# A hybrid encoder trunk on one core: first head by token halves, moved gate products, and factor rows by identity products

## The chip, the cores and the metric

The kernel runs on one core of one Trainium2 chip. Times are device microseconds (us) of one execution of the whole program; of several executions the median is given. A profile is one such execution, taken with the hardware profiler; its span runs from the first to the last instruction of the core.

## The reference, cut to what matters

x is 1024 tokens of 1024 features in float32. Two layers follow each other, each with a mixer and a SwiGLU feed-forward part (width 2816), each part behind an RMS norm and added to x; a last RMS norm ends it.

```python
hn = rmsnorm(x, norm_mix_w[i])                  # x * rsqrt(mean(x*x) + eps) * w
x = x + mlstm_mixer(hn, ...)                    # layer 0;  layer 1: window_attn_mixer
x = x + swiglu(rmsnorm(x, norm_ffn_w[i]), ...)
```

The mLSTM mixer has 4 heads. One product of hn gives for each head q and k (128 features each), v (256), an output gate (256, through a sigmoid), and 16 gate rows for all heads. Each head runs over 8 chunks of 128 tokens, forward and backward, with a state that is carried from chunk to chunk:

```python
s = einsum(q, k) * exp(D - m_t)                 # within the chunk, masked
num = einsum(s, v) + inter * einsum(q, C_prev)  # C_prev: state of the chunks before
h = num / max(|den|, exp(-m_t))
hs = h_fwd + h_bwd
hs = hs * rsqrt(mean(hs*hs) + eps) * norm_w
return (hs * o_gate) @ w_out
```

The attention mixer has 16 heads with windows of 128 tokens, rotary positions and one learned sink value for each head, which enters the maximum and the denominator of the softmax.

## The kernel before, in words

All activations are kept transposed: a tile of x holds 128 features on the partitions and 1024 tokens along the row, so that 8 tiles (`self.x`) hold x. Products go over two halves of 512 tokens. Every float32 operand of a large product is split into a rounded high part and a rest (`split`, `split_scaled`: the high part on ACT, the rest on DVE), and three products (high·high, high·rest, rest·high) make one exact one (`three`). A product of 1024 features into 128 for one half is 24 matmul instructions (`product`). Weights are cut the same way (`cut`: `wh` on ACT at line 187, `wl` on POOL at line 188), and their loads (`feed`, `raw`) run two tiles ahead on the SP queue, in the order that `sources` lists. Most of SBUF is one pool of 46 buffers of 128x1032 words (`unit`); a tile waits for a buffer until an older one is released. x, the normalised tiles (16 buffers, `hnh` and `hnl`), the weights and the per-head data all live there.

The code is written as lists of small steps, which `weave` lays into each other: main steps with filler products between them. The order of the instructions of each engine is fixed when the program is built, by a list scheduler that starts from the order in the code and moves an instruction up where its inputs and buffers are there by estimated times. At run time each engine works its list in order. So code of a later phase can stand early in an engine's list if nothing holds it back: `attn_setup` belongs to the first feed-forward phase (`run`), but its masks and the line-1353 negation of the sinks have tiles of their own in the constant pool, so they need no buffer of the phase before.

Norms: `norm_begin` takes rows R (128 x 1024, the factor of each token on every partition) and `rcol` (the factor of each token down the partitions). `norm_split` (lines 204, 205) makes `hnh` and `hnl` without the factor; products are multiplied by R when they leave PSUM. The sums of squares are summed over partitions by a product with ones (`norm_sums`, line 364), `rsqrt` takes the power -0.5 on POOL (line 353) and two Newton steps on DVE, `spread` (lines 370 to 384) makes R from `rcol`: eight small DVE instructions for 512 tokens build diag(rcol) as a high part and a rest (lines 376, 377), and two products with ones (lines 381, 382) spread it, then ACT copies it into R (line 383). `last_out` uses `spread` for the final norm, in parts of 512, 256 and 256 tokens.

The mLSTM phase (`mlstm`, line 1058): x is loaded (line 240), ACT's list is held to the order of the code while the two halves are split; `norm_direct` makes the sums of squares: the squares of half 0 and two of half 1 on POOL (line 305), six of half 1 on ACT (line 303), the adds on DVE and POOL (lines 306 to 310). The gate rows are 48 products with only 16 output rows (tile `pn`, line 228). Then head 0's features: q, k, and the two gate blocks, each for half 0 then half 1 (`m_in`, 8 products of 24 matmuls), with `norm_sums` and `norm_rows` called between their parts and the gates' long chain (`gates`) advanced at given places (`marks`). From then on the loop over heads weaves the 34 steps of head hh (`m_mix`: `state`, `step`, `prep`) with the 64 feature parts of head hh+1. The last head has no next head: there, with `a, b = 4, 6`, its steps run alone for six steps, while the finished heads 0 and 1 are loaded back (`take_back`, line 711, and their splits at lines 200 and 201), x is loaded again, and the output product (`out_pair`) of heads 0 and 1 fills the rest.

The attention phase (`attn`) weaves 32 units of softmax work with the rotary products of the later query groups (`qs`) by the table `plan`, and with the output products from unit 21 on.

Of the kernel before, what the change touches and what calls it, by code (L numbers as in the profile page):

```python
# [11 lines left out]
F32 = mybir.dt.float32  # L12
# [69 lines left out]
class Trunk:  # L82
# [58 lines left out]
    def sources(self):  # L141
        h = self.h
        cols = lambda src: [src[:, o:o + D] for o in range(0, src.shape[-1], D)]
        out = [h["m_gate"]]
        for u in range(3 * NH):
            out += cols(h["m_in"][u])
        for u in range(4):
            out += cols(h["m_out"][u])
        ffn = [[], []]
        for i in range(2):  # L150
            for f in range(NF):
                ffn[i] += cols(h["ffn_in"][i, f])
            for f0, f1 in FF_CHUNKS:
                ffn[i] += [h["ffn_out"][i, d, :, f0 * P:f1 * P] for d in range(KT)]
        att = []
        for u in range(6):
            att += cols(h["a_in"][u])
        for u in range(4):
            att += cols(h["a_out"][u])
        return out + ffn[0] + att + ffn[1]  # L160
# [134 lines left out]
    def norm_direct(self, half):  # L295
        nc = self.nc
        V, G = nc.vector, nc.gpsimd
        a, b = (self.slab() for _ in range(2))
        for d in range(KT):
            x = self.xv(d, half)  # L300
            sq = (b if d % 2 else a)[:, d // 2 * HALF:(d // 2 + 1) * HALF]
            if half and d < 6:
                nc.scalar.activation(sq, x, AF.Square)
            else:
                G.tensor_tensor(sq, x, x, op=ALU.mult)
        V.tensor_tensor(a[:, :S], a[:, :S], b[:, :S], op=ALU.add)
        G.tensor_tensor(a[:, S:], a[:, S:], b[:, S:], op=ALU.add)
        yield
        V.tensor_tensor(a[:, :S], a[:, :S], a[:, S:], op=ALU.add)
        V.tensor_tensor(self.Rv(half), a[:, :HALF], a[:, HALF:S], op=ALU.add)  # L310
        yield
# [36 lines left out]
    def rsqrt(self, out, ss, n, tag, w):  # L348
        nc = self.nc
        v = self.t([P, w], F32, tag + "v", 2)  # L350
        g = self.t([P, w], F32, tag + "g", 2)
# [18 lines left out]
    def spread(self, t, n):  # L370
        nc = self.nc
        hi, lo = (self.t2(F32R)[:, :n] for _ in range(2))
        for j in range(n // P):
            o = slice(j * P, (j + 1) * P)
            r = self.rcol[:, t // P + j:t // P + j + 1]
            nc.vector.tensor_scalar(hi[:, o], self.ident, r, None, op0=ALU.mult)
            nc.vector.scalar_tensor_tensor(
                lo[:, o], self.ident, r, hi[:, o].bitcast(F32), op0=ALU.mult, op1=ALU.subtract
            )
        rb = self.bank("mx")[:, :n]  # L380
        nc.tensor.matmul(rb, lhsT=self.ones_r, rhs=hi, start=True, stop=False)
        nc.tensor.matmul(rb, lhsT=self.ones_r, rhs=lo, start=False, stop=True)
        nc.scalar.activation(self.R[:, t:t + n], rb, AF.Copy)
        return rb
# [51 lines left out]
    def norm_end(self):  # L436
        sums = lambda: [self.norm_sums(half) for half in range(2)]
        rows = lambda: [self.norm_rows(half) for half in range(2)]
        self.pending = [sums, rows]
# [411 lines left out]
    def m_in(self, hh, t):  # L851
# [4 lines left out]
        def feature(unit, w, half):  # L856
            dst = lambda: t["qk" if unit == 0 else "so"][:, w * S + half * HALF:w * S + (half + 1) * HALF]

            def pairs():
                if w == 0 and half == 0:  # L860
                    t["qk" if unit == 0 else "so"] = self.slab()
                if half == 0:
                    st["w"] = self.w()
                else:
                    self.ahead()
                return self.dense_pairs(st["w"], half)
# [25 lines left out]
        fs = sum((feature(u, w, half) for u in range(2) for w in range(2) for half in range(2)), [])  # L892
        return fs, self.v_parts(value)
# [164 lines left out]
    def mlstm(self):  # L1058
        nc, h = self.nc, self.h
        with ExitStack() as es:  # L1060
# [6 lines left out]
            with self.tc.manual_schedule(engines={mybir.EngineType.Activation}):  # L1067
                sums = [self.norm_direct(half) for half in range(2)]
                for half in range(2):
                    for d in range(KT):  # L1070
                        self.norm_split(d, half)
                        if half and d == 4:
                            next(sums[0])
                    next(gates)
                    next(sums[half])
                next(sums[1])
# [3 lines left out]
            marks = (11, 16, 28, 36, 44)  # L1080
            norms = [lambda: self.norm_sums(0), lambda: self.norm_rows(0), lambda: self.norm_sums(1), lambda: self.norm_rows(1)]
            for i, f in enumerate(ins[0][0]):
                if i in (1, 3, 4, 7):
                    norms.pop(0)()
# [3 lines left out]
            weave(mix[0][0], ins[0][1])  # L1088
            y01, y2 = [[], []], []
            for hh in range(NH):  # L1090
                early, steps, late, y = mix[hh]
                if hh + 1 < NH:
                    weave(steps, ins[hh + 1][0])
                    nxt = mix[hh + 1][0]
                    both = [late[0], nxt[0], late[1], late[2], nxt[1], late[3], late[4], nxt[2], nxt[3]]
                    weave(both, ins[hh + 1][1])
                else:
                    backs = [self.take_back(self.ykeep[j], y01[j]) for j in range(2)]
                    self.load_x(h["x"])
                    back = lambda: self.take_back(self.ykeep[2], y2)()  # L1100
                    idle = [lambda: None]
                    a, b = 4, 6
                    weave(steps[:a] + backs + steps[a:b])
# [233 lines left out]
    def attn_setup(self):  # L1337
# [12 lines left out]
        self.sink = self.const.tile([P, 16], F32, name="sink")  # L1350
        nc.sync.dma_start(self.sink, self.h["sink"])
        self.nsink = self.const.tile([P, 16], F32, name="nsink")
        V.tensor_scalar(self.nsink, self.sink, -1.0, None, op0=ALU.mult)

    def attn(self):
# [8 lines left out]
        with self.phase("a", 6, dict(mm=3, sc=2, tp=2, mx=1)):  # L1364
# [17 lines left out]
            plan = ((0, nq), (4, len(qs) // 3), (11, 2 * len(qs) // 3), (19, len(qs)), (n + 3, len(qs)))  # L1382
# [126 lines left out]
```

## Time and profile before

| | us |
|---|---|
| median of 3 runs | 2332.02 |
| lowest and highest | 2330.37, 2334.89 |
| the profiled execution | 2334.53 |
| its span | 2332.8 |

The mean granted TensorE clock is 0.982 of full speed. PE is busy for 2228.1 us of the span, PE's weight loads for 1826.9, DVE for 1421.6, ACT for 832.8, POOL for 608.7. In the rows further down a time in front is the start from the beginning of the span and the next number the duration, "x8" a count of instructions, and the bracket how long the engine had been idle before and which engine, tile and line released it. A matmul's recorded duration includes the modelled drain, so the spacing of matmuls is read from a run of them: (duration of the run minus one drain) over the count.

### The profile page before, as it was taken

What the parts mean: (1) busy time and instruction counts of PE and PEld (TensorE: products, weight loads), DVE (VectorE), ACT (ScalarE), POOL (GpSimd) and SP (SyncE); (2) the same over time, 40 slices, a digit from 0 to 9 for tenths busy, and PEclk for the clock granted to TensorE, in tenths of its full rate; (3) what the DMA queues carried; (4) which work ended last, traced back from release to release, by engine and by line L of the source; (5) the groups of instructions that cost most, each with busy time, mean ns of one, the idle gap of its engine ahead of it and who ended that gap; (6) DMA issues with size and microseconds to landing.
All of it is one profiled execution on the core that took longest, in us unless ns stands there. A gap on an engine that the chain in (4) does not pass through costs nothing.

```text
span 2332.8 us, 28234 instructions
## 1 busy us (share of the span) xinstructions
PE 2228.1 (96%) x10655; PEld 1826.9 (78%) x10655; DVE 1421.6 (61%) x2603; ACT 832.8 (36%) x1533; POOL 608.7 (26%) x410
## 2 busy tenths in 40 slices
PE   6999998989999999999999998898999999999998
PEld 3889888867888888778878776786788888878887
DVE  5456656678766666592224689878766666653113
ACT  3334445344222222222222577764322222232021
POOL 4312213221111111231343455550111111133043
PEclk9999999998999999999999999999999999999999
DMA  3211114122222222622222444603222222263112
GB/s 114 58 37 46 52 49 145 55 99 82 82 82 82 82 81 77 229 97 86 92 89 85 130 132 135 206 10 116 74 82 81 82 82 82 74 240 119 46 55 73
DMA packets 75961, 216.77 MB, mean 93 GB/s; under 512 B 8320, under 2 KB 14976, under 8 KB 75824
## 3 DMA queue, kind: packets, MB, share of 16 engines
q1 hardware_dynamic: 64216, 177.07, 23.3%
q10 hardware_dynamic: 11608, 37.89, 4.1%
q8 instruction: 84, 1.38, 0.2%
q14 instruction: 53, 0.43, 0.1%
HBM read 159.15 MB, written 55.77 MB: 92 GB/s over the span
## 4 chain that ended last, share of the span: by engine, by line
PE 77%; DVE 8%; issue 5%; DMA 4%; POOL 2%; ACT 2%; SPq 1%; POOLq 0%; ACTq 0%; DVEq 0%
PE mm L532 37%; PE mm L628 18%; PE mm L228 12%; PE mm L476 4%; PE pn L212 2%; DMA raw<-in_a_in_dram 1%; PE sc L1271 1%; POOL wl L188 1%; DVE smd L1286 1%; PE pk L212 1%; DMA slab<-bounce 1%; PE tp L1300 1%; PE mx L1315 1%; ACT e L1280 1%; DVE e L1276 1%
## 5 line engine op out<-in xcount | busy, mean ns | idle before, releaser
L188 POOL TENSOR_TENSOR wl<-raw,wh 128x1024 fp32r<-128x1024 f32 (+2 forms) x96 | 233.7, 2439 | 594.0 <-ACT wh L187 391.2
L628 PE MATMUL mm<-hh,wl 128*128 128x512 f32 (+1 forms) x768 | 289.9, 378 | 4.6 <-POOL wl L188 4.6
L628 PE MATMUL mm<-hh,wh 128*128 128x512 f32 (+1 forms) x768 | 289.0, 379 | 4.3 <-ACT hh L200 3.2
L628 PE MATMUL mm<-hl,wh 128*128 128x512 f32 (+1 forms) x768 | 289.9, 377 | 1.1 <-DVE hl L201 1.1
L579 POOL TENSOR_TENSOR t<-t,R 128x512 f32<-128x512 f32 x44 | 57.4, 1305 | 613.6 <-ACT t L578 613.6
L628 PEld LDWEIGHTS mm<-hh,wh 128*128 128x128 f32 x768 | 145.4, 189 | 34.4 <-ACT hh L200 4.0
L628 PEld LDWEIGHTS mm<-hh,wl 128*128 128x128 f32 x768 | 145.3, 189 | 34.4 <-POOL wl L188 5.9
L628 PEld LDWEIGHTS mm<-hl,wh 128*128 128x128 f32 x768 | 145.5, 189 | 30.3 <-DVE hl L201 1.9
L655 DVE TENSOR_TENSOR x<-x,mm 128x512 f32<-128x512 f32 x80 | 54.6, 685 | 178.2 <-PE mm L628 178.0
L228 PE MATMUL mm<-slab,wh 128*128 128x512 f32 x512 | 152.8, 407 | 6.1 <-ACT wh L187 3.1
L578 ACT ACTIVATE t<-t 128x512 f32<-128x512 f32 x44 | 27.8, 632 | 330.9 <-DVE t L577 330.9
L532 PE MATMUL mm<-f12h,wbh 128*128 128x512 f32 x352 | 138.9, 395 | 0.0
L532 PE MATMUL mm<-f12l,wbh 128*128 128x512 f32 x352 | 138.7, 394 | 0.0
L532 PE MATMUL mm<-f12h,wbl 128*128 128x512 f32 x352 | 138.7, 394 | 0.0
L570 DVE TENSOR_TENSOR t<-mm,t 128x512 f32<-128x512 f32 x44 | 30.4, 691 | 159.9 <-PE mm L532 159.9
L187 ACT ACTIVATE wh<-raw 128x1024 fp32r<-128x1024 f32 (+3 forms) x106 | 102.1, 969 | 71.9 <-DVE hl L201 56.1
L228 PE MATMUL mm<-hnh,wh 128*128 128x512 f32 x416 | 124.6, 399 | 0.9 <-DVE x L655 0.9
L228 PE MATMUL mm<-hnl,wh 128*128 128x512 f32 x416 | 124.5, 401 | 0.0
L228 PE MATMUL mm<-hnh,wl 128*128 128x512 f32 x416 | 124.1, 398 | 0.0
L532 PE MATMUL mm<-f,wah 128*128 128x512 f32 x352 | 113.0, 403 | 10.8 <-DVE x L692 10.8
L532 PE MATMUL mm<-f34h,wd 128*128 128x512 f32 x352 | 117.6, 394 | 0.0
L228 PEld LDWEIGHTS mm<-slab,wh 128*128 128x128 f32 x512 | 95.9, 193 | 26.8 <-ACT wh L187 4.1
(296 smaller groups left out, 5318.7 us busy)
## 6 DMA issues: line engine op xcount, KB each, us to landing
raw<-in_ffn_in_dram SPq DMA_DIRECT2D x88, 512.0 KB
hkeep<-hs ACTq DMA_DIRECT2D x44, 512.0 KB
hraw<-hkeep SPq DMA_DIRECT2D x44, 512.0 KB
raw<-in_ffn_out_dram SPq DMA_DIRECT2D x32, 512.0 KB
raw<-in_m_in_dram SPq DMA_DIRECT2D x24, 512.0 KB
xkeep<-x ACTq DMA_DIRECT2D x24, 512.0 KB
x<-xkeep SPq DMA_DIRECT2D x48, 256.0 KB
bounce<-slab SPq DMA_DIRECT2D x40, 256.0 KB
```

The lines of the kernel that those rows point to most:

```text
L187: nc.scalar.activation(hi[:, c], r[:, c], AF.Copy)
L188: (nc.vector if fast else nc.gpsimd).tensor_tensor(lo[:, c], r[:, c], hi[:, c].bitcast(F32), op=ALU.subtract)
L212: self.nc.tensor.matmul(out, lhsT=l, rhs=r, start=start and i == 0, stop=stop and i == len(jobs) - 1,)
L228: self.nc.tensor.matmul(st["ps"], lhsT=l, rhs=r, start=j == 0, stop=j == len(jobs) - 1)
L476: self.nc.tensor.matmul(st[c], lhsT=l, rhs=r, start=j == 0 and a == 0, stop=j == 1 and a == len(jobs) - 1)
L532: self.nc.tensor.matmul(ps, lhsT=l, rhs=r, start=start and j == 0, stop=stop and j == len(jobs) - 1, skip_group_check=True,)
L570: V.tensor_tensor(u2, pb, p1, op=ALU.add)
L578: A.activation(g0, g0, AF.Silu)
L579: G.tensor_tensor(g0, g0, R0, op=ALU.mult)
L628: nc.tensor.matmul(po, lhsT=l, rhs=r, start=j == 0, stop=j == len(jobs) - 1)
L655: V.tensor_tensor(x, x, po, op=ALU.add)
L1271: T.matmul(ps[:, :n], lhsT=lq, rhs=kk[:, j * S + k0 * P:j * S + (k0 + nk) * P], start=j == 0, stop=j == 1,)
```

## The change

Six edits. (1) The sinks are loaded into a tile of the feed-forward phase's own pool and copied from there. (2) `norm_direct` goes; `norm_half` splits one half and then squares it, all eight squares on ACT, with the adds on DVE. (3) Head 0's first four products run q half 0, k half 0, q half 1, k half 1; the marks are moved to suit. (4) The last head's gate products (`ins[hh][1]`, 32 parts, 96 matmuls) leave the steps of head 2 and stand in the last head's steps 0 to 7; the reload of heads 0 and 1 is issued after the first 16 parts, their splits and the reload of x come after all 32. (5) `spread` multiplies each column of `rcol`, broadcast, with the identity, in plain float32: four products for 512 tokens, no DVE work; `rsqrt`'s scratch tiles have one buffer each. (6) In `attn` the rotary filler that ended at unit 19 ends at unit 21.

```diff
-        for u in range(3 * NH):
+        for u in list(range(3 * NH - 2)) + [3 * NH - 1, 3 * NH - 2]:
             out += cols(h["m_in"][u])
...
+    def norm_half(self, half):
+        V = self.nc.vector
         for d in range(KT):
+            self.norm_split(d, half)
+        q = [self.unit(name="sq") for _ in range(4)]
+        for d in range(KT):
+            o = d % 2 * HALF
+            self.nc.scalar.activation(q[d // 2][:, o:o + HALF], self.xv(d, half), AF.Square)
+        for i, j in ((0, 1), (2, 3), (0, 2)):
+            V.tensor_tensor(q[i], q[i], q[j], op=ALU.add)
+        V.tensor_tensor(self.Rv(half), q[0][:, :HALF], q[0][:, HALF:], op=ALU.add)
...
-        v = self.t([P, w], F32, tag + "v", 2)
-        g = self.t([P, w], F32, tag + "g", 2)
+        v, g = (self.t([P, NC], F32, tag + x, 1)[:, :w] for x in "vg")
...
     def spread(self, t, n):
         nc = self.nc
-        hi, lo = (self.t2(F32R)[:, :n] for _ in range(2))
+        rb = self.bank("mx")[:, :n]
         for j in range(n // P):
-            o = slice(j * P, (j + 1) * P)
-            r = self.rcol[:, t // P + j:t // P + j + 1]
-            nc.vector.tensor_scalar(hi[:, o], self.ident, r, None, op0=ALU.mult)
-            nc.vector.scalar_tensor_tensor(
-                lo[:, o], self.ident, r, hi[:, o].bitcast(F32), op0=ALU.mult, op1=ALU.subtract
+            c = t // P + j
+            nc.tensor.matmul(
+                rb[:, j * P:(j + 1) * P], lhsT=self.rcol[:, c:c + 1].broadcast_to([P, P]), rhs=self.ident,
+                start=True, stop=True,
             )
-        rb = self.bank("mx")[:, :n]
-        nc.tensor.matmul(rb, lhsT=self.ones_r, rhs=hi, start=True, stop=False)
-        nc.tensor.matmul(rb, lhsT=self.ones_r, rhs=lo, start=False, stop=True)
         nc.scalar.activation(self.R[:, t:t + n], rb, AF.Copy)
...
-        fs = sum((feature(u, w, half) for u in range(2) for w in range(2) for half in range(2)), [])
-        return fs, self.v_parts(value)
+        order = [(u, w, half) for u in range(2) for w in range(2) for half in range(2)]
+        if hh == 0:
+            order[1], order[2] = order[2], order[1]
+        fs = [feature(*o) for o in order]
+        return sum(fs[:4], []), sum(fs[4:], []), self.v_parts(value)
...
-                sums = [self.norm_direct(half) for half in range(2)]
                 for half in range(2):
-                    for d in range(KT):
-                        self.norm_split(d, half)
-                        if half and d == 4:
-                            next(sums[0])
+                    self.norm_half(half)
                     next(gates)
-                    next(sums[half])
-                next(sums[1])
...
-            marks = (11, 16, 28, 36, 44)
+            marks = (13, 20, 36, 42, 47)
...
-                if i in (1, 3, 4, 7):
+                if i in (1, 5, 9, 13):
                     norms.pop(0)()
...
-                    weave(steps, ins[hh + 1][0])
+                    weave(steps, ins[hh + 1][0] + (ins[hh + 1][1] if hh + 2 < NH else []))
...
-                    backs = [self.take_back(self.ykeep[j], y01[j]) for j in range(2)]
-                    self.load_x(h["x"])
...
-                    a, b = 4, 6
-                    weave(steps[:a] + backs + steps[a:b])
+                    a, b, o = 4, 8, ins[hh][1]
+                    weave(steps[:a], o[:16])
+                    backs = [self.take_back(self.ykeep[j], y01[j]) for j in range(2)]
+                    weave(steps[a:b], o[16:])
+                    for f in backs:
+                        f()
+                    self.load_x(h["x"])
...
-        self.sink = self.const.tile([P, 16], F32, name="sink")
-        nc.sync.dma_start(self.sink, self.h["sink"])
-        self.nsink = self.const.tile([P, 16], F32, name="nsink")
-        V.tensor_scalar(self.nsink, self.sink, -1.0, None, op0=ALU.mult)
+        raw = self.t([P, 16], F32, "sink", 1)
+        nc.sync.dma_start(raw, self.h["sink"])
+        self.sink, self.nsink = (self.const.tile([P, 16], F32, name=n) for n in ("sink", "nsink"))
+        V.tensor_copy(self.sink, raw)
+        V.tensor_scalar(self.nsink, raw, -1.0, None, op0=ALU.mult)
...
-            plan = ((0, nq), (4, len(qs) // 3), (11, 2 * len(qs) // 3), (19, len(qs)), (n + 3, len(qs)))
+            plan = ((0, nq), (4, len(qs) // 3), (11, 2 * len(qs) // 3), (21, len(qs)), (n + 3, len(qs)))
```

## Rows read from the trace of the kernel before

**Rows 1.** The page, busy time by engine (busy us, share, instructions).

```profile
PE   2228.1 (96%) x10655; PEld 1826.9 (78%) x10655; DVE 1421.6 (61%) x2603; ACT 832.8 (36%) x1533; POOL 608.7 (26%) x410
```

**Rows 2.** Busy time by stage, the start (stage, length, engines, granted clock, DMA).

```profile
0.00:25.00 25.00, 6.93 (x12) 1.18 (x12) 8.99 (x11) 16.48 (x25) 22.30 (x26) 1.00 0.72 256
50.00:55.00 5.00, 5.00 (x13) 3.88 (x12) 2.52 (x5) 0.60 (x1) 0.00 (x0) 0.50 0.09 16
```

**Rows 3.** The timeline of the start, DVE, ACT, POOL and SP (start, duration, work).

```profile
4.83 8.93 POOL L305 TENSOR_TENSOR slab<-x 128x512 f32<-128x512 f32 x8
...
8.84 8.05 ACT L204 ACTIVATE hnh<-x,nw 128x512 fp32r<-128x512 f32 x12 [0.18 <-DMA x<-in_x_dram]
...
12.86 0.33 SPq L1351 DMA_DIRECT2D sink<-in_sink_dram  x1
...
16.80 3.21 ACT L303 ACTIVATE slab<-x 128x512 f32<-128x512 f32 x6
19.01 0.17 DVE L1353 TENSOR_SCALAR nsink<-sink 128x16 f32<-128x16 f32 x1 [11.15 <-DMA sink<-in_sink_dram]
19.10 9.57 DVE L205 SCALAR_TENSOR_TENSOR hnl<-x,nw,hnh 128x512 fp32r<-128x512 f32 x8
...
19.92 1.04 ACT L187 ACTIVATE wh<-raw 128x1024 fp32r<-128x1024 f32 x1
...
29.72 2.07 DVE L205 SCALAR_TENSOR_TENSOR hnl<-x,nw,hnh 128x512 fp32r<-128x512 f32 x3
```

**Rows 4.** The timeline, PE alone, from the gate rows to head 0's last feature.

```profile
27.14 3.19 PE L228 MATMUL pn<-hnh,wl 128*16 128x512 f32 x7
...
37.91 1.78 PE L228 MATMUL mm<-hnh,wh 128*128 128x512 f32 x7
...
49.49 0.76 PE L381 MATMUL mx<-t,ones 128*128 128x512 f32 x1 [3.07 <-DVE t L376]
...
92.73 0.40 PE L228 MATMUL mm<-hnh,wl 128*128 128x512 f32 x1
92.97 1.05 PE L907 MATMUL mx<-slab,slab 128*128 128x128 f32 x8
```

**Rows 5.** Busy time by stage, head 2's steps and the last head.

```profile
310.00:360.00 50.00, 50.00 (x269) 42.75 (x268) 27.68 (x81) 20.27 (x44) 7.82 (x4) 1.00 0.10 32
...
395.00:400.00 5.00, 3.99 (x28) 3.26 (x27) 3.40 (x14) 3.56 (x9) 1.14 (x1) 1.00 0.97 330
400.00:405.00 5.00, 2.56 (x16) 2.06 (x14) 4.81 (x9) 3.76 (x9) 4.78 (x4) 0.88 0.93 366
405.00:410.00 5.00, 2.50 (x6) 1.92 (x7) 3.30 (x10) 2.83 (x5) 1.68 (x1) 0.50 0.00 2
410.00:415.00 5.00, 5.00 (x15) 3.80 (x15) 0.69 (x1) 0.26 (x1) 3.04 (x2) 0.60 0.34 108
```

**Rows 6.** The timeline of the last head: SP's loads, POOL, and PE's first output product.

```profile
378.54 1.82 SPq L711 DMA_DIRECT2D slab<-ykeep  x4
...
391.61 6.60 SPq L240 DMA_DIRECT2D x<-in_x_dram  x12
...
398.86 5.92 POOL L201 TENSOR_TENSOR slab<-slab,slab 128x512 fp32r<-128x512 f32 x4 [18.12 <-ACT slab L200]
...
408.30 2.93 PE L228 MATMUL mm<-slab,wh 128*128 128x512 f32 x6 [1.18 <-ACT wh L187]
```

**Rows 7.** Lines 376 and 377 over the whole span (count, ns min/median/max).

```profile
L376 DVE TENSOR_SCALAR t<-ident,rcol x40: 273/280/286, 40.6 to 2324.7; 128x128 fp32r<-128x128 f32 x40
...
L377 DVE SCALAR_TENSOR_TENSOR t<-ident,rcol,t x40: 340/344/898, 41.0 to 2325.1; 128x128 fp32r<-128x128 f32 x40
```

**Rows 8.** The timeline, PE behind a factor row: feed-forward part, and the end.

```profile
558.85 0.80 PE L532 MATMUL mm<-f23h,wah 128*128 128x512 f32 x1 [3.40 <-ACT t L559]
...
2325.00 0.39 PE L381 MATMUL mx<-t,ones 128*128 128x256 f32 x1 [2.73 <-DVE t L376]
```

**Rows 9.** Busy time by stage, attention between rotary filler and output filler.

```profile
1450.00:1460.00 10.00, 5.21 (x25) 3.78 (x24) 8.57 (x20) 6.01 (x16) 6.54 (x5) 0.92 0.20 58
```

More of the change, by code (lines that the diff above doesn't have):

```diff
@@ L293, in norm_square_row @@
         self.seen = [n + 1 for n in self.seen]
[L295 to L298, printed above, removed]
+    def norm_half(self, half):
+        V = self.nc.vector
         for d in range(KT):
[L300 to L311, printed above, removed]
+            self.norm_split(d, half)
[6 more added lines that the diff above has]
+        V.tensor_tensor(self.Rv(half), q[0][:, :HALF], q[0][:, HALF:], op=ALU.add)
     def norm_add(self, d, half):
@@ L437, in norm_end, with norm_all_rows @@
         sums = lambda: [self.norm_sums(half) for half in range(2)]
-        rows = lambda: [self.norm_rows(half) for half in range(2)]
-        self.pending = [sums, rows]
+        self.pending = [sums, self.norm_all_rows]
+    def norm_all_rows(self):
+        for half in range(2):
+            self.norm_rows(half)
     def settle(self):
@@ L862, in pairs @@
                 if half == 0:
-                    st["w"] = self.w()
-                else:
+                    st[w] = self.w()
+                elif hh or unit or w:
                     self.ahead()
-                return self.dense_pairs(st["w"], half)
+                return self.dense_pairs(st[w], half)
             def done(ps):
@@ L1079, in mlstm @@
             mix = [self.m_mix(hh, st[hh], self.ykeep[hh] if hh < NH - 1 else None) for hh in range(NH)]
-            marks = (11, 16, 28, 36, 44)
-            norms = [lambda: self.norm_sums(0), lambda: self.norm_rows(0), lambda: self.norm_sums(1), lambda: self.norm_rows(1)]
-            for i, f in enumerate(ins[0][0]):
-                if i in (1, 3, 4, 7):
+            marks = (13, 20, 36, 42, 47)
+            norms = sum(([lambda h=h: self.norm_sums(h), lambda h=h: self.norm_rows(h)] for h in range(2)), [])
+            for i, f in enumerate(ins[0][0] + ins[0][1]):
+                if i in (1, 5, 9, 13):
                     norms.pop(0)()
@@ L1087, in mlstm @@
                 f()
-            weave(mix[0][0], ins[0][1])
+            weave(mix[0][0], ins[0][2])
             y01, y2 = [[], []], []
@@ L1092, in mlstm @@
                 if hh + 1 < NH:
-                    weave(steps, ins[hh + 1][0])
+                    weave(steps, ins[hh + 1][0] + (ins[hh + 1][1] if hh + 2 < NH else []))
                     nxt = mix[hh + 1][0]
                     both = [late[0], nxt[0], late[1], late[2], nxt[1], late[3], late[4], nxt[2], nxt[3]]
-                    weave(both, ins[hh + 1][1])
+                    weave(both, ins[hh + 1][2])
                 else:
-                    backs = [self.take_back(self.ykeep[j], y01[j]) for j in range(2)]
-                    self.load_x(h["x"])
                     back = lambda: self.take_back(self.ykeep[2], y2)()
                     idle = [lambda: None]
-                    a, b = 4, 6
-                    weave(steps[:a] + backs + steps[a:b])
+                    a, b, o = 4, 8, ins[hh][1]
[5 more added lines that the diff above has]
+                    self.load_x(h["x"])
                     weave(steps[b:] + [back] + late[:1] + 4 * idle + late[1:] + 4 * idle, self.out_pair(y01))
```

## The prediction

> **What bounds the kernel now.** I read the page's busy times first: PE works 2228.1 of 2332.8 us [rows 1], so only about 105 us of idle PE, plus what slow clock costs, can be won, and the change takes no large product away. Next come the busy times by stage, to find where PE stands still. The first 25 us hold only 6.93 us of PE [rows 2], and the stretch 395 to 410 only 3.99, 2.56 and 2.50 of 5 us each [rows 5]. Then the timelines of those two stretches say what PE waited for. In the start the reader is to see a chain that has nothing to do with PE: DVE stands still for 11.15 us until 19.01 for the load of the sinks, a constant of the attention phase [rows 3]; behind it in DVE's list are the rests `hnl`, without which no product is complete. They then take 9.57 us for 8, because POOL is working beside them; later three take 2.07 us, 0.69 each [rows 3].
>
> **The start, edits 1 to 3.** ACT becomes the engine that sets the pace, so I walk along it. Its 12 last splits took 8.05 us, 0.67 each; the fifth began at 8.84 [rows 3], so half 0 is split at 8.84 + 4 x 0.67 = 11.5, as before, since x's loads are not touched. Squares on ACT cost 3.21 / 6 = 0.535 us [rows 3]: eight are 4.3 us, done at 15.8. Half 1's splits: 5.4 us, 21.2. Its squares: 25.5. The first feature weight `wh` follows, 1.04 us [rows 3], at 26.5 (before: 20.96, so this part is later than now). POOL's eight squares, 8.93 us [rows 3], go, so POOL is free for `wl`, and DVE runs at 0.69 a rest, 11 us for 16, well inside ACT's time. DVE's adds (three of 1024 and one of 512 columns a half) hide behind ACT's half 1; half 1's own end at about 28.6, and R for half 1 is needed only when the third product leaves, about 39.
>
> PE: the gate rows of half 0 need all of half 0's splits and finish while ACT is at half 1. Those of half 1 wait for the last `hnh` at 21.2; 17 of their 24 matmuls are still to come then. Spacing was 0.43 us there (3.19 us for 7, less a drain) and 0.23 later (1.78 for 7) [rows 4], so they end between 25 and 28.6. I take 28 for the first feature matmul, nearer the slow spacing because PE idles between splits just before; it was 37.91.
>
> From there to the end of the eighth feature took 92.97 - 37.91 = 55.1 us [rows 4]. 192 matmuls of 0.233 are 44.7. [...] 28 + 44.7 + 5.9 = 78.6. I add 2 us for waits that the new order will have of its own, 80.6 against 92.97: **-12.4 us**. Bounds: no new wait and the early start, -16; a wait of the old size with its slow clock, 5.6 us, and a worse gate end, -6. The gates' own long chain (two trips through DRAM) starts from R half 1, 12 us earlier than now, and so keeps pace with the features.
>
> The sinks' wait is not removed but moved (edit 1): load and two small DVE instructions now stand in the first feed-forward phase, behind the release of the mLSTM phase's scratch. The load took from 12.86 to 19.01, 6.15 us for 8 KB, behind weights and x [rows 3]. I price it at 0, since PE has output products there, and keep +6 as the other end.
>
> **The last head, edit 4.** Before, the three windows from 395 leave 5.95 us idle; the granted clock of 0.88, 0.50 and 0.60 takes 0.3 + 1.25 + 2.0 = 3.55 more [rows 5]. That is 9.5 us. 96 matmuls x 0.233 = 22.4 us of gate products now fill it. PE's total is the same; they are taken from head 2's steps, where PE was never idle and DVE had 27.68 of 50 us [rows 5]. There some 62 us of PE work becomes 40, while DVE keeps 62 x 0.554 less four evictions, about 32: 80% busy, a chain of small waits; I charge 2 us. At the end of the gate products the heads 0 and 1 must be split before `out_pair` can begin. POOL's four rests take 5.92 us [rows 6]; the buffers for them come free only as the last gate products release the normalised tiles, so I charge 2.5 us of PE waiting. 9.5 - 2 - 2.5: **-5 us**, with -9.5 (all hidden) and the rival below as ends.
>
> **Spread, edit 5.** Eight DVE instructions, 4 x (0.280 + 0.344) with overlapping starts about 1.9 us for 512 tokens, go out of the chain from `rcol` to R [rows 7]. PE pays: four plain float32 products of 128 columns are recorded as 8 matmuls; the nearest row, four such products of head 0's scores, took 1.05 us [rows 4], against 0.47 for the two wide ones: +0.55 a half. In both feed-forward parts PE stands 3.40 us behind ACT, which waited for R (the second, 3.41, is alike) [rows 8]: -1 each, since one-buffer scratch puts the two halves' Newton steps behind each other and gives half back. Attention's norm has no wait: +1.1. The last two parts' spreads: PE waited 2.73 us at the end [rows 8], -0.8 there, +0.5 for the hidden ones. Sum **-1.2**, between -4 (no give-back) and +4 (all paid, nothing won).
>
> **Plan, edit 6.** Between the two fillers PE was busy for 5.21 of 10 us, but DVE for 8.57 [rows 9]. Filler brings DVE work too, so little can be won: **-1**, from -5 to +4 (the last query group is then written two units later, still ahead of its use).
>
> **Sum.** -12.4 - 5 - 1.2 - 1 = -19.6. The durations are of an execution of 2334.53, a tenth of a per cent over the median 2332.02; the terms don't feel that. 2332.0 - 19.6 = 2312.4, I say **2312**.
>
> **Rivals.**
> *The start does not move* (8%). If the sinks' wait hid another of the same length, for instance x's landing, edit 1 brings nothing. Against it: `hnh` was complete at 16.9 while DVE stood still [rows 3]. With ACT's longer list and a new wait of 5.6 us the start gains 6 instead of 12.4: 2318.
> *The sinks wait in a worse place* (10%). DVE's list stands behind an 8 KB load again, now in front of feed-forward work. Up to 6.15 us at the price of [rows 3]: 2312 + 6 = 2318. [...]
> *The last head starves* (7%, the one that ends slower). Now heads 0 and 1 and x are reloaded while the last products on the normalised tiles run. Buffers were already short: 12 of x's 16 loads could be issued only from 391.61 [rows 6]. If the reloads must wait for the 16 normalised buffers, they start only when the gate products end, and PE's list stands at its first output product, steps behind it. From the first reload to that product took 408.30 - 378.54 = 29.8 us [rows 6]; with 3.3 of slow clock and the old 9.5 taken off, the last head costs +23.6 instead of -5: 2332 - 14.6 + 23.6 = 2341. It decides if the first reload is issued less than some 10 us before the last gate product. Against it: four reload buffers were free at 378.54, with all normalised tiles alive [rows 6].
> *The last head half* (17%): splits and x come late, PE waits some 7 us more, 2319.
> *Better* (8%): both stalls vanish and attention gains, 2300.
>
> **How the numbers follow.** Forecast 50%: 2306 to 2318. The cases of 2318 and 2319 hold 35%, 2300 has 8%, 2341 has 7%. The range 2302 to 2325 leaves out the slower case and most of the better one, and takes in the unknown prices. A measurement of this kernel can tell about 0.2%, 4.7 us: faster is under 2327.3, slower over 2336.7. The slower case gives 0.06 to slower; cases of 2318 with a second loss, and the rest of the starved one, give 0.06 to no change; 0.88 to faster.
>
> **What would show it.** In the changed profile: no DVE wait for the sinks at the start; ACT without a gap to about 25.5; the first feature matmul near 28 and head 0's scores near 80; PE busy over 90% between 370 and 405 and at full granted clock; the L559 wait under 3 us; no line 376. Wrong if PE's list stands more than 5 us at the first output product, if the scores begin after 88, or if a wait for the sinks shows in front of feed-forward work.

## The result, and the profile after

| | before | after |
|---|---|---|
| median, us | 2331.59 (4 runs) | 2319.97 (4 runs) |
| the profiled execution | 2334.53 | 2319.65 |
| ratio, 95% interval | | 0.9947 [0.9929, 0.9964] |

The change makes the kernel 11.6 us faster; 19.6 were forecast. The profiled execution of before lies 2.9 us over its median and that of after 0.3 under, so that two profiles differ by 14.9 where the medians differ by 11.6. Differences of two profiles below are read with that in mind, and verdicts come from the medians. The changed kernel was timed only here, and the experiments later; where it is set beside one of them, the medians can be off by the 1 us or so by which the kernel before drifted.

Where the time went is seen by following PE through its landmarks:

| start of, us | before | after | difference |
|---|---|---|---|
| first feature product | 37.91 | 25.61 | -12.3 |
| head 0's scores | 92.97 | 90.72 | -2.3 |
| head 2's scores | 277.25 | 274.24 | -3.0 |
| first feed-forward product | 524.71 | 514.55 | -10.2 |
| its first down product | 965.02 | 950.96 | -14.1 |
| second feed-forward product | 1623.05 | 1610.21 | -12.8 |
| end of the span | 2332.8 | 2317.9 | -14.9 |

The start wins 12 us and has lost 10 of them 65 us later. The last head wins some 7 and each feed-forward part some 4 (the second down product starts 16.6 earlier, 2063.35 against 2046.71). The attention gives 1 to 2 back, as do the last 270 us, but that is less than such stretches scatter: in the profiles of the fourteen kernels of this record the stretch from the first down product to the second feed-forward product took 657.3 to 663.0 us, and the one from the second down product to the end 268.4 to 271.7. PE's busy time fell by only 5.3 us, from 2228.1 [rows 1] to 2222.8.

**The start.** The busy time by stage of after (columns as in [rows 2]), to set beside its two stretches and beyond them:

```profile
0.00:25.00 25.00, 16.57 (x54) 5.66 (x55) 17.08 (x26) 20.82 (x35) 4.23 (x13) 1.00 0.71 255
50.00:55.00 5.00, 5.00 (x23) 4.07 (x22) 3.53 (x4) 3.49 (x4) 3.34 (x2) 1.00 0.67 213
55.00:60.00 5.00, 2.27 (x10) 1.50 (x8) 4.69 (x11) 0.00 (x0) 1.42 (x1) 1.00 0.00 0
60.00:65.00 5.00, 2.03 (x5) 1.56 (x6) 3.89 (x14) 0.00 (x0) 0.00 (x0) 0.73 0.00 0
65.00:70.00 5.00, 5.00 (x15) 3.44 (x14) 1.09 (x11) 0.00 (x0) 0.00 (x0) 0.58 0.00 0
```

The first 25 us hold 16.57 us of PE instead of 6.93, and the slow clock of 50 to 55 is gone. But from 55 to 65 PE works 4.30 of 10 us, and then, from 65 to 70, at a granted clock of 0.58. The timeline of after, PE alone, answers to [rows 4]:

```profile
25.61 1.78 PE L228 MATMUL mm<-hnh,wh 128*128 128x512 f32 x7
...
31.88 2.07 PE L368 MATMUL mx<-ident,rcol 128*128 128x128 f32 x8 [2.63 <-DVE rcol L350]
...
42.95 1.13 PE L368 MATMUL mx<-ident,rcol 128*128 128x128 f32 x8 [1.38 <-DVE rcol L350]
...
62.97 0.26 PE L788 MATMUL mx<-ident,msmall 64*1 64x64 f32 x1 [5.70 <-DVE msmall L784]
...
90.72 1.05 PE L902 MATMUL mx<-slab,slab 128*128 128x128 f32 x8
```

All three waits stand at small products: two factor spreads and the gates' first transpose (line 788, of a 64x1 column). In PE's list they stand behind 15, 39 and 96 of head 0's 192 feature matmuls, and feature products whose inputs are long there stand behind them. What made the inputs of the second and the third late is seen in the timeline of after, DVE and POOL:

```profile
38.63 2.38 POOL L188 TENSOR_TENSOR wl<-raw,wh 128x1024 fp32r<-128x1024 f32 x1
38.70 2.34 DVE L348 SCALAR_TENSOR_TENSOR ng<-rcol 128x4 f32<-128x4 f32 x1 [1.13 <-POOL rcol L346]
...
42.24 0.16 DVE L348 SCALAR_TENSOR_TENSOR ng<-rcol 128x4 f32<-128x4 f32 x1
...
51.66 4.76 POOL L188 TENSOR_TENSOR wl<-raw,wh 128x1024 fp32r<-128x1024 f32 x2 [10.65 <-ACT wh L187]
51.75 0.69 DVE L862 SCALAR_TENSOR_TENSOR slab<-mm,R 128x512 f32<-128x512 f32 x1 [1.46 <-PE mm L228]
52.36 1.80 DVE L757 TENSOR_SCALAR slab<-slab 64x128 f32<-64x128 f32 x1
54.09 2.42 DVE L765 TENSOR_SCALAR slab<-slab 64x128 f32<-64x128 f32 x1
```

The same instruction on 128x4 elements takes 0.16 us, and 2.34 when POOL's subtraction has begun 0.07 before it: it ends at 41.04, and POOL's at 41.01. Two instructions of the gate chain take 1.80 and 2.42 beside two such subtractions. The first factor's way is another: its power on POOL (line 346) stands behind POOL's subtraction of 25.49 to 28.20 and then takes 2.00 us, where the second factor's takes 1.01.

**The sinks.** All instructions on the tile, over the whole span of after, and what DVE waited for:

```profile
L1343 SPq DMA_DIRECT2D sink<-in_sink_dram x1: 328/328/328, 460.5 to 460.5; - x1
L1345 DVE COPY sink<-sink x1: 718/718/718, 462.1 to 462.1; 128x16 f32<-128x16 f32 x1
...
  DMA sink<-in_sink_dram: 2.8, 1
```

DVE stands 2.8 us at 462 instead of 11.15 at 19 [rows 3], while PE works on output products. The load, issued at 460.50, was there by 462.1: the later load was a quicker one, 1.6 us against 6.15. The DMA engines had been idle from 455 to 460 (share 0.00); in before they were busy all through the load's 6.15 us (share 1.06 from 12.86 to 19.01). That this made the difference is an inference; no run tests it alone.

**The last head.** Busy time by stage of after, against [rows 5]:

```profile
395.00:400.00 5.00, 5.00 (x28) 4.25 (x27) 4.94 (x5) 1.57 (x4) 3.85 (x3) 1.00 0.87 277
400.00:405.00 5.00, 5.00 (x29) 4.30 (x29) 3.69 (x14) 2.64 (x6) 0.00 (x0) 1.00 0.99 352
...
410.00:415.00 5.00, 3.14 (x15) 2.25 (x14) 4.89 (x5) 2.59 (x4) 2.38 (x1) 1.00 0.75 252
```

The stall and its slow clock are gone. The timelines of SP and PE, against [rows 6]:

```profile
364.23 7.44 SPq L703 DMA_DIRECT2D slab<-ykeep  x4
...
394.54 9.35 SPq L240 DMA_DIRECT2D x<-in_x_dram  x16
...
397.25 1.09 PE L228 MATMUL mm<-slab,wh 128*128 128x512 f32 x4
...
414.63 0.51 PE L212 MATMUL pk<-vx,slab 128*128 128x258 f32 x2 [1.86 <-ACT slab L200]
...
422.40 0.39 PE L212 MATMUL pk<-vx,slab 128*128 128x258 f32 x1 [2.15 <-DVE slab L201]
```

The reload of heads 0 and 1 is issued 32 us before the last gate product (396.66), and the first output product follows it without a wait. Two waits of 1.86 and 2.15 in the head's own steps are left; before had the second of them too, 1.86 at 429.54.

**The factor rows.** PE of after in the first feed-forward part and at the end, against [rows 8]:

```profile
544.56 1.13 PE L368 MATMUL mx<-ident,rcol 128*128 128x128 f32 x8 [0.84 <-DVE rcol L350]
551.01 0.50 PE L524 MATMUL mm<-f12h,wbl 128*128 128x512 f32 x1 [0.44 <-DVE wbl L201]
...
2310.01 1.19 PE L368 MATMUL mx<-ident,rcol 128*128 128x128 f32 x4 [2.30 <-DVE rcol L350]
```

### The profile page after: what moved, and what is told of

Same layout as the page of the kernel before. It is cut to its first block, busy times and chain, and to the rows that moved or that the text cites. A ratio compares the mean times of both kernels' runs of the same rounds, so it can differ in the third digit from the quotient of the medians.

```text
span 2317.9 us, 28270 instructions
## 1 busy us (share of the span) xinstructions
PE 2222.8 (96%) x10713; PEld 1825.4 (79%) x10713; DVE 1403.9 (61%) x2526; ACT 839.3 (36%) x1544; POOL 593.8 (26%) x398
## 3 DMA queue, kind: packets, MB, share of 16 engines
q8 instruction: 84, 1.38, 0.2%
## 4 chain that ended last, share of the span: by engine, by line
PE 78%; DVE 9%; issue 4%; DMA 3%; POOL 3%; ACT 2%; SPq 0%; POOLq 0%; DVEq 0%; ACTq 0%
PE mm L524 36%; PE mm L620 17%; PE mm L228 14%; PE mm L468 4%; PE pn L212 2%; PE mx L1307 1%; PE tp L1292 1%; PE sc L1263 1%; DMA slab<-bounce 1%; PE pk L212 1%; DMA raw<-in_a_in_dram 1%; DVE slab L1133 1%; DMA slab<-ykeep 1%; DVE e L1268 1%; POOL wl L188 1%
## 5 line engine op out<-in xcount | busy, mean ns | idle before, releaser
L1280 POOL TENSOR_TENSOR e<-e,smd 128x768 f32<-128x768 f32 (+1 forms) x64 | 89.3, 1397 | 101.7 <-DVE smd L1279 62.4
```

The costliest lines, as they stand in the source:

```text
L1280: G.tensor_tensor(e[:, j:j + 2, :n], e[:, j:j + 2, :n], d.unsqueeze(2).broadcast_to([P, 2, n]), op=ALU.mult,)
```

## The experiments

"Before" in a ratio is the kernel before, timed on the same chip at the same time; its medians there lie between 2332.16 and 2332.98.

**Three parts alone.** Each kernel is the one before with some of the edits: 1 to 3 (the start), 4 (the last head), 5 (the spread).

```diff
 start_alone: + norm_half, halves swapped for head 0, marks (13, 20, 36, 42, 47), sinks late
 last_alone:  + gate products of head 3 in its own steps, a, b = 4, 8
 spread_alone: + spread by rcol x identity, one-buffer scratch in rsqrt
```

> The kernel before with edits 1 to 3 alone (sinks later, squares on ACT, first head by halves with its marks). Theory A (the start's gain is given back inside the start: PE stands behind the factor rows and, longest, at the gates' first transpose, and runs at the half clock behind each wait): head 0's scores begin 2 to 4 us earlier than the 92.97 of before, and the whole is 2 to 4 us faster, about 2329. Theory B (the start is worth its forecast 12 us and another edit of the change costs 5 or more): scores near 81, the whole about 2319.

> The kernel before with edit 4 alone (the last head's gate products moved into its own steps). Theory A: the stretch from the last value product to the feed-forward part loses its whole 9.5 us of stall, and head 2's steps and head 3's first steps give back 2 to 3: about 7 us faster, 2324.5. Theory B (the forecast's sizes: 2 us in head 2's steps and 2.5 at the end of the gate products): 5 us faster, 2326.5.

> The kernel before with edit 5 alone (factor rows by identity products, one buffer for the scratch of the power). Theory A (both feed-forward waits of 3.4 us nearly go, and PE's dearer products cost 1 us only in attention's norm; the start wins some of its 3 us wait): 6 to 8 us faster, about 2324.5. Theory B (the forecast: a third of each wait goes and PE pays the rest): 1 us faster, 2330.5, within 2 us of before.

| | median, us | ratio | head 0's scores |
|---|---|---|---|
| start alone | 2332.40 (12 runs) | 1.0001 [0.9993, 1.0009] | 90.86 |
| last head alone | 2326.17 (12) | 0.9976 [0.9968, 0.9985] | 91.79 |
| spread alone | 2325.59 (12) | 0.9976 [0.9968, 0.9985] | 90.07 |

Last head and spread, -6.0 and -6.6, are the whole change; the part that was to bring most brings nothing. The start edits do bring the scores 2.1 us earlier, as theory A said, but not the 2 to 4 us of the whole; of the last head theory B has the time, 0.3 from 2326.5, and of the spread theory A has it, near the lower end of its 6 to 8 us. PE's waits at the start, of the kernel with the start edits alone:

```profile
33.42 0.51 PE L375 MATMUL mx<-t,ones 128*128 128x512 f32 x1 [2.91 <-DVE t L370]
...
42.79 0.80 PE L375 MATMUL mx<-t,ones 128*128 128x512 f32 x1 [2.72 <-DVE t L370]
63.10 0.26 PE L790 MATMUL mx<-ident,msmall 64*1 64x64 f32 x1 [3.55 <-DVE msmall L786]
```

They stand at the three places of after and come to 9.2 us, there to 9.7, so the new spread did not make them. How the spread wins 6.6 is seen in the stretch behind the factor row. First the busy time by stage of the kernel before (its row of the wait itself is in [rows 8]), then that of the spread alone:

```profile
555.00:560.00 5.00, 1.60 (x5) 0.97 (x5) 4.14 (x7) 4.46 (x6) 2.13 (x2) 0.74 0.00 0
560.00:565.00 5.00, 5.00 (x15) 3.90 (x14) 3.30 (x4) 2.53 (x3) 0.39 (x1) 0.58 0.27 108
```

```profile
545.00:550.00 5.00, 4.43 (x24) 3.40 (x22) 4.07 (x11) 3.00 (x4) 2.24 (x2) 1.00 0.00 0
550.00:555.00 5.00, 4.74 (x25) 4.07 (x26) 2.28 (x5) 2.18 (x3) 1.39 (x2) 1.00 0.02 3
```

The wait of 3.40 also cost clock: 5 us at 0.58 are 2.1 us lost. Waits of 0.83 and 0.44 in its place cost none (1.00 from 545 to 565). That is 3.4 + 2.1 - 1.3 - 0.5 for the dearer spread = 3.7 for the first feed-forward part, some 3.2 by the same sum for the second (there the clock of before was 0.67 from 1660 to 1665, which is 1.65 us lost), and 0.4 at the end. The profiles of the fourteen kernels bear it out: from its first product to its first down product the first part takes 440.0 us on average with the old spread and 435.8 with the new, the second 439.3 and 436.5. The spread alone also brings the scores 2.9 us earlier: the 3.07 of [rows 4] are gone, and one wait of 1.55 at the gates' first transpose is new. All this adds up to some 10, more than the 6.6 of the medians, and what takes the rest is not shown.

**Both together, and the plan.** The kernel before with edits 4 and 5; and the changed kernel with `(21, len(qs))` put back to `(19, len(qs))`.

> The kernel before with edits 4 and 5 alone (last head, spread); the start, the sinks and the plan as before. Theory A (the start edits bring nothing, since PE's fixed order puts new waits where the old one was): the two parts add up, 2332.2 - 6.0 - 6.6 = 2319.6, within 1.5 of the changed kernel. Theory B (the 2 us by which the changed kernel's first scores come earlier are kept to the end, and are only hidden when the start is changed alone): 2322 to 2323, slower than the changed kernel by 2 to 3.

> The changed kernel with edit 6 undone (the third filler of the attention ends at unit 19 again). Theory A (the trace: the attention phase got 1.5 us longer in the changed kernel, and 2.84 us of PE waiting at 1381.82, 1.66 at 1455.68 and 3.21 at 1486.62 are new): 1 to 2 us faster than the changed kernel, 2318 to 2319. Theory B (the forecast: the later end of the filler gains about 1): 2321.

Last head and spread: 2320.30 (5 runs), ratio 0.9940 [0.9927, 0.9953], as theory A had it: without the start edits and the plan the kernel is as fast as the changed one. With the plan put back: 2317.94 (6 runs, 2313.16 to 2321.60), 0.9930 [0.9918, 0.9943]. That is 2 us under the changed kernel by the medians, 4 by the ratios, with intervals that overlap, so the plan is not settled; theory A, 1 to 2 us faster without it, fits. The stretch of [rows 9] lies some 13 us earlier now. First the busy time by stage with the plan put back, then that of after:

```profile
1440.00:1450.00 10.00, 5.21 (x19) 3.74 (x18) 7.77 (x17) 4.89 (x12) 5.62 (x5) 0.83 0.26 65
```

```profile
1440.00:1450.00 10.00, 8.43 (x47) 6.98 (x47) 8.16 (x26) 8.91 (x28) 6.71 (x6) 1.00 0.76 274
```

The later end of the filler does fill the gap, but the gap has only moved: from 1450 to 1460 and from 1480 to 1490 PE works 6.39 and 6.74 us in after, and 8.24 and 8.41 with the plan put back.

**Who makes the small inputs late: POOL.** The changed kernel, with the weight rests of head 0 on DVE.

```diff
-                    st[w] = self.w()
+                    st[w] = self.w(fast=hh == 0)
...
-                    self.ahead()
+                    self.ahead(fast=hh == 0)
```

> The changed kernel with head 0's weight rests (wl, and the first v weight's) subtracted on DVE in two halves each instead of on POOL. Theory A (DVE's small instructions of the gate chain and of the factors take 1.8 to 2.4 us instead of 0.2 because POOL subtracts beside them, and so the gate maxima reach PE late): no DVE instruction of lines 345 to 350 and 757 to 765 over 0.3 us, PE's wait of 5.70 us at the gates' first transpose falls to 2 or less, that of 2.63 at the first factor product to about 1; with the clock that it costs, 3 to 6 us faster than the changed kernel, 2314 to 2317. Theory B (DVE is the bound of the chain itself: 1.4 us more work for each weight makes it as late as before): the waits stay within 1 us of what they were, 2319 to 2321.

2313.33 us (4 runs), 0.9913 [0.9900, 0.9926]: 6.6 us under the changed kernel. The timeline of this run, DVE and PE:

```profile
47.18 0.21 DVE L757 TENSOR_SCALAR slab<-slab 64x128 f32<-64x128 f32 x1
47.31 0.21 DVE L765 TENSOR_SCALAR slab<-slab 64x128 f32<-64x128 f32 x1
...
54.01 0.21 PE L788 MATMUL mx<-ident,msmall 64*1 64x64 f32 x1 [1.91 <-DVE msmall L784]
...
79.05 1.05 PE L902 MATMUL mx<-slab,slab 128*128 128x128 f32 x8
```

The two instructions fall from 1.80 and 2.42 to 0.21 each, the wait at the transpose from 5.70 to 1.91, and head 0's scores start at 79.05, where the prediction had 80.6. Theory A holds, by a little more than it said. In PE's list the second factor product and the transpose stand where they stood, behind 39 and 96 feature matmuls; the first factor product moved, from 15 to 21, so that its wait (2.63, now 0.65) is not a test of POOL alone. Not all that the scores win lasts: they come 11.7 us earlier and the whole is 6.6 faster. Some of it goes right behind the scores, where PE works 6.6 us from 85 to 95, at a mean clock of 0.75; the like stretch of after, 95 to 105, has 7.9, at 0.83.

The same edit on the kernel before:

> The kernel before with nothing but head 0's weight rests subtracted on DVE instead of POOL. Theory A (it frees what the start edits gain, and alone has little to free: one wait of 3.07): 2328 to 2331. Theory B (POOL beside DVE costs the kernel before as much as the changed one, which gained 6.6 by it): 2325 to 2327.

2327.59 (8 runs), 0.9976 [0.9966, 0.9986]; scores at 86.13. That lies between the theories, nearer to B: the kernel before paid 5 us for it too. Its wait of 3.07 [rows 4], 0.72 in this run, was this effect, as DVE and POOL of before show:

```profile
45.41 0.16 DVE L356 TENSOR_TENSOR ng<-ng,nv 128x4 f32<-128x4 f32 x1
45.53 2.36 POOL L188 TENSOR_TENSOR wl<-raw,wh 128x1024 fp32r<-128x1024 f32 x1 [0.94 <-ACT wh L187]
45.61 2.29 DVE L357 SCALAR_TENSOR_TENSOR rcol<-ng,rcol 128x4 f32<-128x4 f32 x1
```

**Who makes PE wait for them: the order of its list.** Two versions hold PE's list to the code's order while head 0's features run. In the first, norms stand at parts (1, 10, 11, 18) and marks at (19, 26, 50, 54, 60); there R still holds the sums of squares when head 0's first product is multiplied by it, so that this product is scaled by another row, against the "nothing is computed otherwise" of its expectation; the instructions are the same. The second puts the last three matmuls of the first product behind half of the second one, and both factor sums first:

```diff
+            first = ins[0][0] + ins[0][1]
+            first.insert(11, first.pop(7))
+            with self.tc.manual_schedule(engines={mybir.EngineType.PE}):
...
+                    if i in (1, 8, 11, 15):      # sums 0, sums 1, rows 0, rows 1
...
+            marks = (16, 22, 46, 49, 55)
```

> The changed kernel, with PE's list in head 0's features held to the order of the code, the factor products at parts 10 and 18 (5 and 13 before) and the gates' PE work at marks 50, 54 and 60 (36, 42, 47). Nothing is computed otherwise. Theory A: PE no longer stands 2.6, 1.4 and 5.7 us, nor the slow clock behind them; head 0's scores begin near 78 (90.72 in the changed kernel), and the whole is 9 to 12 us faster than the changed kernel, 2308 to 2311. Theory C (the gates' chain on DVE and its trips through DRAM are the limit, not PE's order): PE's waits go from the transposes to the scores, which need the gates' rows; the whole gains under 4 us, 2316 or more.

2315.14 (6 runs), 0.9934 [0.9920, 0.9947], between the theories, with the scores at 87.71. PE no longer stands at the gates' transposes (0.0 us before lines 788 and 789), but part of the wait comes back at the chain's end:

```profile
81.12 0.76 PE L909 MATMUL pk<-rows,sel 128*128 128x512 f32 x1 [1.80 <-DMA rows<-rkeep]
```

Marks this late make the gates' rows late, which is why the second version has them earlier.

> The changed kernel with PE's list held to the order of the code while head 0's features run. In that order all factor sums come first, head 0's first product is finished only after half of the second one, behind the factor products that it needs, and the gates' transposes stand where their inputs were ready in the run with PE's list held before. Theory A (the waits at the start come from where the scheduler put the small products into PE's list): PE without a wait over 0.7 us from 26 to 70, the gates' first transpose waits under 1 us, head 0's scores at 84 to 87, total 5 to 9 us faster than the changed kernel, 2311 to 2315. Theory B (the inputs are late whatever the order: each wait is only moved to the next small product): scores at 89 or later, 2318 to 2320.

2303.43 (4 runs), 0.9872 [0.9859, 0.9885]: 29.5 us faster than before and 16.5 faster than the changed kernel, beyond theory A in both time and scores. Busy time by stage, and from the timeline the last write of DVE that the transpose needs, and the two landmarks on PE:

```profile
25.00:75.00 50.00, 50.00 (x236) 39.80 (x234) 30.82 (x76) 13.46 (x20) 15.72 (x7) 1.00 0.18 49
```

```profile
59.10 0.14 DVE L784 COPY msmall<-slab 32x1 f32<-32x1 f32 x1
...
61.90 0.21 PE L788 MATMUL mx<-ident,msmall 64*1 64x64 f32 x1
...
75.90 1.05 PE L902 MATMUL mx<-slab,slab 128*128 128x128 f32 x8
```

PE works 50 of 50 us at full clock. POOL still slows DVE's gate chain (two of its instructions took 2.32 and 2.36 beside it). What the transpose needs is written at 59.10, 3.6 us earlier than the 62.68 of after; but PE comes to it at 61.90, behind 138 of the 192 feature matmuls. Behind 96, as in after, it would have come at about 61.9 - 42 x 0.233 = 52.1 and stood 7 us (an estimate from this run's rows). The two factor products stand behind 33 and 45. So the place in the list takes the wait away. The hold and the new places were changed together; the places without the hold were not run.

**Are the start edits needed for that?** The same held list on the kernel before with the start edits alone, and on the kernel before without any.

> The kernel before with edits 1 to 3 (the start) and PE's list held to the code's order while head 0's features run, as in the run of the changed kernel with the held list; spread, last head and plan as before. Theory A (the start edits are worth the forecast 12.4 or more, but the order that the scheduler gave PE's small products took it back): scores at 78 to 82, 2333 - 29.5 + 12.6 = 2316, 2314 to 2319, where the start edits alone gave 2332.4. Theory B (the held order pays only with the spread by identity products, because the old spread's eight DVE instructions for 512 tokens make the factor late again): scores at 85 to 88, 2322 to 2326.

> The kernel before with nothing but PE's list held to the code's order while head 0's features run (with the same places for factors and gates). Theory A (before, the first feature product stands at 38 because of the sinks and of POOL's squares, so that the order can win back only the wait of 3.07 and its slow clock): scores at 88 to 90, 2327 to 2330. Theory B (the order is what counts and the start edits are still worth nothing): the same as with the start edits and the held order.

| | list by scheduler | list held |
|---|---|---|
| start as before | 2332.77 | 2340.48 (6 runs), 1.0032 [1.0020, 1.0045] |
| start edits | 2332.40 | 2319.34 (5), 0.9948 [0.9936, 0.9961] |

The ratios are to the kernel before timed beside each run; the 2332.40 was taken earlier, when before took 2332.16. With the held list the start edits are worth 21 us, and 13.4 against the kernel before, about the forecast 12.4 (scores at 76.65, earlier than theory A's 78; the time 0.3 over its range); with the scheduler's list they are worth nothing. The held list alone loses 7.7, which neither theory had, so that much of the 21 is a loss avoided. Its timeline shows why:

```profile
60.75 4.78 POOL L188 TENSOR_TENSOR wl<-raw,wh 128x1024 fp32r<-128x1024 f32 x2 [12.68 <-ACT wh L187]
60.99 2.32 DVE L767 TENSOR_TENSOR slab<-slab 64x128 f32<-64x128 f32 x1
...
63.34 2.34 DVE L768 TENSOR_TENSOR slab<-slab 64x128 f32<-64x128 f32 x1
...
69.94 0.69 DVE L874 TENSOR_TENSOR slab<-mm,R 128x512 f32<-128x512 f32 x1
...
70.78 3.33 PE L228 MATMUL mm<-hnh,wh 128*128 128x512 f32 x7 [6.28 <-DVE slab L874]
```

In DVE's list the eviction of a feature (line 874) stands behind the gate chain that POOL delays; PE waits 6.28 us for that eviction, and the next seven products take 3.33 instead of 1.78; the mean clock from 65 to 75 is 0.67.

**Both cures at once:** the held list and the weight rests on DVE.

> The changed kernel with both: PE's list held, and head 0's weight rests on DVE. Theory A (both take away the same waits, so that the second adds little): 2301 to 2304 beside 2303.4 for the held list alone. Theory B (they add up: 6.6 on top of 16.5): 2297. Theory C (DVE, 7 us more of work before 80, makes the features' evictions late): 2306 or more.

2310.69 (4 runs), 0.9907 [0.9894, 0.9921]: the time of theory C, 7 us worse than the held list alone. But what is late is not a feature's eviction, as C had it: the weight rest itself is, behind the gate chain in DVE's list:

```profile
57.66 0.67 DVE L188 TENSOR_TENSOR wl<-raw,wh 128x512 fp32r<-128x512 f32 x1
...
58.39 3.20 PE L228 MATMUL mm<-hnh,wl 128*128 128x512 f32 x7 [3.07 <-DVE wl L188]
```

The version with the held list and POOL's subtractions where they were beats both kernels and is the fastest that was run.

## Why the prediction was right, and which of its steps failed

2320.0 is 8 over the forecast 2312 and inside 2302 to 2325, and faster it is. That it came out inside is in part luck: the start, the largest term, brought nothing, and the spread and the last head brought 6.4 more than was said.

*The start, -12.4: measured 0.* Its first half held: the splits and squares on ACT let the first feature product go at 25.61 (28 was said), and the sinks' wait is gone from the start. The step that failed is "I add 2 us for waits that the new order will have of its own", with "and so keeps pace with the features" for the gate chain. The 5.9 that its sum adds to the features is a term that no run shows: with the list held the way from the first feature product (26.04) to the scores (75.90) took 49.86 us, 5.1 over the 44.7 of the features, and in after 65.1, 20.4 over. The waits were 2.63, 1.38 and 5.70, 9.7 us, with slow clock behind the first and the last (0.66 from 30 to 35, 0.58 from 65 to 70). The gate chain began 8.6 us earlier than before (50.01 against 58.57), not 12, and what the transpose needs came only 4.4 earlier (62.68 against 67.10), while the features ran 12 us ahead. Both halves of the cause are shown: without POOL beside DVE the scores come at 79.05 and the time falls by 6.6, about half of the forecast gain; with PE's list in another order, while POOL slows DVE as before, they come at 75.90 and it falls by 16.5. With that order the start edits bring 13.4 against the kernel before. By its own test, scores after 88, this step was wrong. The outcome was that of the rival "the start does not move", by another mechanism than it named and below even its 6 us. Its sign was in [rows 4]: the 3.07 us in front of a factor product were not the factor row's own work alone, since one of six equal instructions, 0.16 us each, took 2.29.

*The last head, -5: measured -6.0.* The mechanism held: the 9.5 are gone, the steps of head 2 and head 3's early work pay 0.61 and 1.55 (2 was charged). The 2.5 at the end of the gate products were not paid there; 1.86 and 2.15 in the last steps were, of which before had paid 1.86. The rival that starves fell, for the reason given against it: four reload buffers were free.

*The spread, -1.2: measured -6.6.* The term mis-sized is "-1 each" at the feed-forward parts. The wait shrank by 2.1 instead of 1, and the step left out the clock: 2.1 us more behind the first wait (5 us at 0.58) and 1.65 behind the second (5 us at 0.67), though the same bill had been put on the wait of the start: its 5.6 us are the 3.07 of [rows 4] and half of the 5.00 at a clock of 0.50 in [rows 2]. It also left out that those 3.07 would go: the spread alone brings the scores 2.9 us earlier. The end, -0.8, was -0.4.

*The plan, -1: not settled;* the medians say +2, within the noise. *The sinks, 0:* right, with a wait of 2.8 at 462, under output products rather than in the feed-forward phase. The load took 1.6 us there instead of 6.15, with the DMA engines idle before it (share 0.00).

The sum by measured parts is 0 - 6.0 - 6.6 = -12.6, and the change measured -11.6.

## What to carry to other kernels

Here 12.3 us at the first feature product became 2.3 at the scores: the early start was worth only what the next small product in PE's fixed list let through. List those products (factor sums, transposes, spreads) with the time at which each input is ready, and give each a place behind products that are ready anyway. A wait is priced with the clock behind it (here 2.1 us behind one of 3.40, none behind 0.83 and 0.44). Before moving POOL work next to a chain of small DVE instructions, compare the longest with the median of each line: a 0.16 that was once 2.29 (line 357 of before) pointed to the culprit. Here an order won more than moving the work to DVE, 16.5 us against 6.6, and both at once made that work itself late: PE waited 3.07 us for a weight rest.

## What the runs showed of the hardware

Small DVE instructions, on 128x4 or 64x128 elements in SBUF, that met POOL's subtraction of two SBUF tiles (2.36 to 2.40 us for 128x1024) did not slow down by a share in these traces: they ended when POOL's ended. In after line 348 took 2.34 us instead of 0.16 and ended at 41.04, POOL's subtraction at 41.01; lines 757 and 765, 0.21 each with the weight rests on DVE, took 1.80 and 2.42 and ended at 54.16 and 56.51, beside two subtractions from 51.66 to 56.42. In before line 357 took 2.29 instead of 0.16 and ended at 47.90, POOL's at 47.89. An eviction with one input in PSUM, at 51.75 beside the first of those two subtractions, took its usual 0.69. Lines 348 and 357 have two SBUF inputs, lines 757 and 765 one; what sets them apart from the eviction is not shown.

The bill of a wait in clock was uneven: 5.70 us of waiting in after and 3.40 in before were followed by 5 us at 0.58 (65 to 70, 560 to 565), two waits of 0.83 and 0.44 in the spread alone by none (1.00 from 545 to 565). In the kernel with the held list, two of 0.53 and 1.08 (at 82.96 and 84.54) were followed by 10 us at a mean clock of 0.67 (85 to 95).
